# GpSimd's remainders given to VectorE in the latent loop and the band, with the band's sums of exponentials, and the band's casts of weights to ScalarE

## The chip, the core and the metric

The kernel runs on one core of a Trainium2 chip. Its time is the device time of one execution in microseconds (us), the median over runs; lower is better. Five engines work on their own instruction streams and meet at semaphores: TensorE (PE, matmuls; its weight loads are PEld), VectorE (DVE), ScalarE (ACT), GpSimd (POOL) and SyncE (SP, which issues the transfers here). On-chip memory is SBUF; matmuls write into PSUM, in which a "bank" of 512 float32 columns is what one output tile of this kernel holds.

## The reference

A two-layer encoder trunk over 1024 positions of width 1024, all float32. Layer 0 mixes with two groups of heads side by side, layer 1 with a banded attention; each is followed by a SwiGLU feed-forward.

```
layer 0: u = rms_norm(h); proj = u @ w_in -> c_q (384), c_kv (256), k_r (32), q_b, k_b, v_b
  latent:         q_a = rms_norm(c_q) @ w_uq, rotary on the last 32 of 96
                  kv  = rms_norm(c_kv) @ w_ukv; 8 heads; softmax over (s // 64) <= (t // 64)
  stick-breaking: 8 heads of 64, weights from cumulative sums of log_sigmoid(-z)
  h += concat(o_a, o_b) @ w_out
layer 1: 16 heads of 64; each chunk of 64 attends to itself and the 8 before it,
         scores + bias[clip(rel)], softmax, h += o @ w_out
both:    h += (silu(u @ w_gate) * (u @ w_up)) @ w_down        (d_ff 2816), u = rms_norm(h)
end:     rms_norm(h)
```

## The kernel before

**Numbers in two parts.** Every matmul operand is kept as two parts: `hi`, the value rounded to the type fp32r, and `lo`, the remainder, `src - hi` (also fp32r). A product of two such operands is three matmuls (`mm3`, L286 to L291: hi·hi, hi·lo, lo·hi). `split` (L259) makes both parts: `round_to` (L250 to L254) does the rounding as a cast on ScalarE ("act", L252) or VectorE (L254), and `rest` (L256, L257) the subtraction on GpSimd ("pool") or VectorE ("dve"). `weight` (L276) loads a weight by transfer into `wr` tiles of 128x512 and splits it into `wh` and `wl`; each of the three kinds has four buffers. So in the profile L252 and L254 are roundings, and L257 is a remainder, and tile names tell which: `wl<-wr,wh` of weights, `u<-c,u`, `u<-t,u`, `u<-ld,u` of activations.

**Stages.** By the profile's clock: stick-breaking attention to about 415 us (in its last pass, p = 3, the generator `prepare` fills in and makes the first latent tiles); the latent attention loop to about 600; the output projection and the first feed-forward to about 1345, of which 705 to 1290 is in an order written out by hand ("pinned", all on helper line L76) and 1290 to 1345 is its tail, which adds the residual (L719), normalizes (L312, L336, L337) and already loads the band's first weights; the band attention, pairs of heads p = 0 to 7 at about 57 us each, to about 1850, with the output projection's first half (`half(0)`) woven into the last pairs; then the second feed-forward and the end.

**The latent loop** (L1283 to L1302). For each p of 0 to 3, attention of two heads is woven with the projections of the next p: `mla_keys` (L1001) multiplies c_kv's tiles with `w_uk`, scales by a vector into a `c` tile (L1011), splits it (64 rows), and copies the shared rotary key beside it (L1013 on ScalarE, L1014 on VectorE: `lo[64:96] = kc[0:32]`, a cast of 32 rows). `mla_query` (L1017) does the same for queries, with the rotary turn (L997 to L999) into a 96-row `c` tile. `mla_max` (L1048) computes the scores once for their maxima: matmuls L1058 into a two-bank tile `z` (two buffers), whose maximum VectorE takes (L1060), which frees the banks. `mla_attend` (L1111) computes scores again (L1129 to L1131) into the same `z` buffers, ScalarE exponentiates (L1132), and the weighted values go to `o` (L840).

**Sums of exponentials.** `soft_step` (L1065) adds each key block's exponentials to a running tile `b` (L1081): on GpSimd, except where `dest[2]` is set (the last pair of each loop, p = 3 and p = 7), where it is VectorE. `soft_finish` (L1093) sums `b` over partitions by matmuls with ones (L1097), inverts (L1099 to L1102) and scales (L1103).

**The band.** `band_project` (L1139) loads two weights per pair, with the cast on VectorE and the remainder on GpSimd (VectorE for p = 0), and splits the projected `t` tiles on ScalarE and VectorE. `band_max` (L1170) makes scores (L1184) and VectorE adds the bias and takes the maximum in one instruction (L1187, reading and freeing `z`). `band_attend` (L1194) makes scores (L1210, L1211), VectorE adds the bias into an `a` tile (L1212, which frees `z`), ScalarE exponentiates in place (L1213), then the sum (L1081).

**Order.** Outside the pinned part a tile scheduler orders each engine's instructions by its own model when the program is built, and `weave` interleaves attention with filling projections by given costs. So changing an instruction's engine also changes the order round it. An engine runs its instructions in order: one that waits holds up all behind it.

Of the kernel before, what the change touches and what calls it, by code (L numbers as in the profile page):

```python
# [158 lines left out]
class Trunk:  # L159
    def __init__(self, ctx, tc, a):  # L160
# [12 lines left out]
        self.pending = []  # L173
        self.late = []

    def nm(self, s):
        self.n += 1
        return f"{s}{self.n}"
# [77 lines left out]
    def rest(self, eng, lo, src, hi):  # L256
        self.eng(eng).tensor_tensor(lo, src, hi.bitcast(F32), ALU.subtract)  # L257

    def split(self, src, hi, lo, eng_hi="act", eng_lo="pool"):  # L259
        self.round_to(eng_hi, hi, src)  # L260
        self.rest(eng_lo, lo, src, hi)

    def wtile(self, t, part, dt):
        if t:
# [8 lines left out]
            self.nc.sync.dma_start(tiles[-1][:, :w], src[:, c:c + w])  # L273
        return tiles

    def weight(self, src, n=1024, eng_hi="act", eng_lo="pool", into=None, raws=None):  # L276
        parts = []
        for c in range(0, n, HALF):
            w = min(HALF, n - c)
            raw = raws[c // HALF] if raws else self.raws(src[:, c:c + w], w)[0]  # L280
            hi, lo = into[c // HALF] if into else (self.wtile(0, "h", F32R), self.wtile(0, "l", F32R))
            self.split(raw[:, :w], hi[:, :w], lo[:, :w], eng_hi, eng_lo)
            parts.append((hi, lo))
        return Weight(parts)
# [129 lines left out]
    def out_loads(self, o_row, last, parts):  # L414

        for k in range(KD):
            if k != last:
                t, hi, lo = self.load(o_row[k]), self.unit(F32R), self.unit(F32R)
                self.split(t, hi, lo, "act", "pool" if k % 2 else "dve")
                parts[k] = hi, lo  # L420
                yield

    def out_half(self, hf, w, parts, resid, ks, s, h_d, early=0):

        o = [x[0] for x in parts], [x[1] for x in parts]
        ahead, raws, wts = [], [], []
        for m in range(KD):
            while len(ahead) < min(AHEAD, KD - m):
                ahead.append(self.load(resid(hf, m + len(ahead))))
            x, h = ahead.pop(0), self.unit()  # L430
            for n in range(m + len(wts), min(m + early + 1, KD)):
                raw = raws.pop(0) if raws else None
                wts.append(self.weight(w[n], eng_lo="dve" if early else "pool", raws=raw))
            if early and m + early + 1 < KD:
                raws.append(self.raws(w[m + early + 1]))
            ps = self.bank()
            yield from self.dense(ps, wts.pop(0), o, ks)
            self.nc.vector.tensor_tensor(h, ps, x, ALU.add)
            self.nc.sync.dma_start(h_d[hf][m], h)
            s.h[hf].append(h)  # L440
            s.acc[hf] = self.square_sum(s.acc[hf], h)
# [623 lines left out]
    def soft_step(self, lag, scores, cs, st, vt, j, first, last, dest):  # L1065
        x = {}

        def front():
            ex = x["ex"] = self.tmp("a")
            scores(ex)  # L1070
            if first:
                st["ex"] = ex
            else:
                old = st["ex"]
                if "esum" not in st:
                    st["esum"] = self.tmp("b")
                    if cs.start:
                        self.nc.scalar.copy(st["esum"][:, :, 0:cs.start], old[:, :, 0:cs.start])
                else:
                    old = st["esum"]  # L1080
                self.eng("dve" if dest[2] else "pool").tensor_tensor(st["esum"][:, :, cs], old[:, :, cs], ex[:, :, cs],  # L1081
                                                                     ALU.add)

        def back():
            if first:
                st["o"] = self.out_bank()
            self.weighted(st["o"], vt, j, x["ex"], cs, first, last)
            if last:
                self.soft_finish(st["o"], st["esum"], *dest)

        self.step(front, *[lambda: None] * (lag - 1), back)
# [47 lines left out]
    def band_project(self, p, s, out, hfs=(0, 1)):  # L1139

        nc, a = self.nc, self.a
        for i in range(2):
            w = self.weight(a["w_qk1"][2 * p + i], eng_hi="dve", eng_lo="dve" if p == 0 else "pool")
            for hf in hfs:
                ps = self.bank()
                yield from self.dense(ps, w, s.u[hf], range(KD))
                t = self.tmp("t")
                nc.vector.scalar_tensor_tensor(t, ps, 1.0 if i else 0.125, s.r[hf], ALU.mult, ALU.mult)
                for e in range(2):
                    x, y = self.unit(F32R), self.tmp("y", F32R) if i and e == 0 else self.unit(F32R)  # L1150
                    rh = slice(64 * e, 64 * e + 64)
                    rl = slice(64 - 64 * e, 128 - 64 * e)
                    self.split(t[rh, :], x[rh, :], (x[rl, :], y[0:64, :])[i == 0], "act", "dve")
                    if i == 0:
                        nc.sync.dma_start(x[rl, :].bitcast(F32), x[rh, :].bitcast(F32))
                    else:
                        nc.scalar.copy(y[0:64, :], t[rh, :])
                        nc.gpsimd.memset(y[64:68, :].bitcast(F32), 1.0)
                    out[i][e].append((x, y))
# [83 lines left out]
    def mixer0(self, h_d):  # L1243
        nc, a = self.nc, self.a
# [4 lines left out]
        with self.phase("mix0", MIX0_TEMPS):  # L1249
# [5 lines left out]
            raw = [[[], []], [[], []]]  # L1255
# [15 lines left out]
            for p in range(4):  # L1271
                nxt = ([[], []], [[], []], [])
                if p < 2:
                    vw = [a["w_vb"][2], a["w_vb"][3]]
                    fill, cost = self.chain(self.sb_project(p + 1, u, nxt), vgen(vw, 1, [p])), 31.0
                elif p == 2:
                    fill, cost = self.chain(self.sb_project(3, u, nxt), self.rope_key(u)), 31.0
                else:
                    fill, cost = prepare(), 73.0
                self.weave(self.ending(self.sb_attend(p, proj, vts[p], o_d)) if p == 3 else  # L1280
                           self.sb_attend(p, proj, vts[p], o_d), 9.24, fill, cost)
                proj = nxt
            for p in range(4):  # L1283
                nxt = ([[], []], [[], []])
                first, second = (self.mla_attend(p, hf, mla, va[p], o_d) for hf in range(2))
# [19 lines left out]
    def mixer1(self, u, h_d, h2_d):  # L1305
        a = self.a
        o_d = self.spill("o1_")
        out = Stream()
        half = lambda hf, *e: self.out_half(hf, a["w_out1"], o_p[hf], lambda hf, m: h_d[hf][m], list(range(KD)), out,
                                            h2_d, *e)  # L1310
        with self.phase("band", BAND_TEMPS):
            vts = [[] for _ in range(8)]
            vgen = lambda g, hf: self.values([a["w_v1"][2 * g], a["w_v1"][2 * g + 1]], u, 4, KD, 1,
# [185 lines left out]
```

## Time and profile before

| what | value |
|---|---|
| median of 3 runs | 2574.17 us (2573.54 to 2580.01) |
| the profiled execution: time, span | 2573.97 us, 2571.9 us |
| mean granted TensorE clock | 0.993 |
| TensorE busy | 2483.8 us (97%), 11710 matmuls |
| VectorE busy | 1885.4 us (73%), 3074 instructions |
| ScalarE busy | 1170.4 us (46%), 2028 |
| GpSimd busy | 518.1 us (20%), 489 |
| remainders of weights on GpSimd (L257) | 122.9 us, 95, mean 1.299 us |
| sums on GpSimd, `b<-b,a` (L1081) | 110.1 us, 80, mean 1.376 us |

A row of a timeline gives start, duration, engine, line, operation, tiles written and read, shapes and, in brackets, how long the engine had stood idle and what it waited for. A row of a group of instructions gives count, total busy us and mean ns of one, and behind the second bar the idle time before them. Busy times of TensorE are of overlapping matmuls whose ends are modelled.

### The profile page before, as it was taken

Reading aid. Unit: us, or ns where it says so; the run is one execution under the profiler, and the core shown is the slowest. Engines: PE = TensorE matmul, PEld = TensorE weight load, DVE = VectorE, ACT = ScalarE, POOL = GpSimd, SP = SyncE. Lnnn points to the kernel's source line nnn. Section 1 sums busy time; section 2 is a strip of 40 time slices with the busy share of each in tenths; the row PEclk is TensorE's granted clock in tenths of the full one; section 3 lists DMA queues with packets and bytes.
Section 4 is the critical chain, followed back from the end, with each engine's and each line's share of the span. In section 5 each row is a group of like instructions: output and inputs, shape, how many; then the busy total and the mean of one; then the engine's idle time right before and its main releaser. Section 6 shows DMA issues by size and latency. Waiting matters only on the chain.

```text
span 2571.9 us, 33553 instructions
## 1 busy us (share of the span) xinstructions
PE 2483.8 (97%) x11710; PEld 1938.0 (75%) x11710; DVE 1885.4 (73%) x3074; ACT 1170.4 (46%) x2028; POOL 518.1 (20%) x489
## 2 busy tenths in 40 slices
PE   7999998999999999999999999999999999999997
PEld 6766765557778888888878777776777888888886
DVE  6888888666787667677775777777788666667775
ACT  4677676444454344433253344434445443443324
POOL 3333324663000000000031333435300000000004
PEclk9999998999999999999999999999999999999999
DMA  4221100015524343475651222223543433447661
GB/s 140 62 64 54 54 17 29 27 62 164 172 84 150 131 145 125 146 277 184 241 182 54 83 87 80 78 74 111 164 160 116 155 115 131 145 149 255 212 222 70
DMA packets 179432, 319.70 MB, mean 124 GB/s; under 512 B 20544, under 2 KB 36800, under 8 KB 179264
## 3 DMA queue, kind: packets, MB, share of 16 engines
q1 hardware_dynamic: 179264, 317.56, 37.0%
q8 instruction: 93, 1.52, 0.2%
q14 instruction: 75, 0.61, 0.1%
HBM read 222.58 MB, written 84.41 MB: 119 GB/s over the span
## 4 chain that ended last, share of the span: by engine, by line
PE 71%; DVE 10%; DMA 2%; issue 1%; ACT 1%; POOL 0%; DVEq 0%; SPq 0%; POOLq 0%; ACTq 0%
PE z L76 24%; PE mm L76 12%; PE o L76 6%; PE mm L289 5%; PE mm L290 5%; PE mm L291 5%; PE o L840 4%; DVE u L76 2%; PE z L1210 1%; PE z L1184 1%; PE z L1211 1%; DVE u L312 1%; PE z L1097 1%; PE z L1129 1%; DMA wr<-in_w_down 1%
## 5 line engine op out<-in xcount | busy, mean ns | idle before, releaser
L76 PE MATMUL z<-u,wh 128*128 128x512 f32 x976 | 302.3, 390 | 7.1 <-DVE u L76 6.5
L76 PE MATMUL z<-u,vh 128*128 128x512 f32 x976 | 301.7, 390 | 4.0 <-DVE u L76 4.0
L289 PE MATMUL mm<-u,wh 128*128 128x512 f32 x720 | 288.7, 401 | 3.0 <-DVE c L998 1.8
L257 POOL TENSOR_TENSOR wl<-wr,wh 128x512 fp32r<-128x512 f32 (+2 forms) x95 | 122.9, 1299 | 806.8 <-ACT wh L252 739.4
L290 PE MATMUL mm<-u,wh 128*128 128x512 f32 x720 | 284.5, 395 | 0.0
L291 PE MATMUL mm<-u,wl 128*128 128x512 f32 x720 | 282.9, 393 | 0.0
L76 PE MATMUL mm<-u,wh 128*128 128x512 f32 x720 | 223.4, 392 | 4.5 <-ACT wh L76 4.5
L76 PEld LDWEIGHTS z<-u,wh 128*128 128x128 f32 x976 | 183.1, 188 | 48.1 <-DVE u L76 9.4
L76 PEld LDWEIGHTS z<-u,vh 128*128 128x128 f32 x976 | 182.9, 188 | 44.2 <-ACT u L76 5.6
L76 PE MATMUL z<-u,wl 128*128 128x512 f32 x488 | 190.0, 389 | 0.5 <-DVE wl L76 0.5
L76 PE MATMUL z<-u,vl 128*128 128x512 f32 x488 | 189.9, 389 | 0.0
L289 PEld LDWEIGHTS mm<-u,wh 128*128 128x128 f32 x720 | 135.5, 188 | 55.7 <-issue 29.7
L76 PEld LDWEIGHTS mm<-u,wh 128*128 128x128 f32 x720 | 134.7, 188 | 35.5 <-ACT wh L76 6.8
L291 PEld LDWEIGHTS mm<-u,wl 128*128 128x128 f32 x720 | 135.6, 188 | 27.3 <-issue 0.9
L290 PEld LDWEIGHTS mm<-u,wh 128*128 128x128 f32 x720 | 135.8, 189 | 26.7 <-issue 3.0
L840 PE MATMUL o<-a,u 128*64 128x512 f32 (+3 forms) x768 | 155.3, 476 | 0.0
L76 PE MATMUL mm<-u,vh 128*128 128x512 f32 x496 | 152.7, 389 | 0.0
L257 POOL TENSOR_TENSOR u<-wr,u 128x512 fp32r<-128x512 f32 x8 | 10.9, 1373 | 669.5 <-ACT u L252 669.5
L76 PE MATMUL mm<-u,wl 128*128 128x512 f32 x360 | 140.8, 391 | 0.8 <-DVE wl L76 0.5
L1081 POOL TENSOR_TENSOR b<-b,a 128x512 f32<-128x512 f32 (+3 forms) x80 | 110.1, 1376 | 130.0 <-ACT a L1213 101.2
L1212 DVE TENSOR_TENSOR a<-z,bias 128x1024 f32<-128x1024 f32 (+3 forms) x96 | 78.1, 822 | 75.8 <-PE z L1211 70.1
L76 ACT CAST vh<-vr 128x512 fp32r<-128x512 f32 (+1 forms) x166 | 95.8, 577 | 81.3 <-DVE vr L76 30.4
(249 smaller groups left out, 5917.1 us busy)
## 6 DMA issues: line engine op xcount, KB each, us to landing
u<-f_t SPq DMA_DIRECT2D x144, 256.0 KB, 5.0
vr<-in_w_up SPq DMA_DIRECT2D x88, 256.0 KB, 4.5
wr<-in_w_gate SPq DMA_DIRECT2D x88, 256.0 KB, 3.6
f_t<-x SPq DMA_DIRECT2D x72, 256.0 KB, 2.0
wr<-in_w_out SPq DMA_DIRECT2D x64, 256.0 KB, 3.0
f_t<-e SPq DMA_DIRECT2D x54, 256.0 KB, 3.5
ld<-f SPq DMA_DIRECT2D x54, 256.0 KB, 5.1
h<-u SPq DMA_DIRECT2D x48, 256.0 KB, 2.2
```

What stands on the lines that cost most here:

```text
L76: return lambda *a, **k: self.tc.keep_in_program_order(f(*a, **k))
L257: self.eng(eng).tensor_tensor(lo, src, hi.bitcast(F32), ALU.subtract)
L289: mm(out, wh, xh, start=first, stop=False, skip_group_check=onto)
L290: mm(out, wh, xl, start=False, stop=False, skip_group_check=onto)
L291: mm(out, wl, xh, start=False, stop=last, skip_group_check=onto)
L312: self.eng(eng).tensor_tensor(acc, acc, sq, ALU.add)
L840: self.nc.tensor.matmul(o[rh, cs], vt[j // 4][:, j % 4, rh], w[:, e, cs], start=first, stop=last)
L1081: self.eng("dve" if dest[2] else "pool").tensor_tensor(st["esum"][:, :, cs], old[:, :, cs], ex[:, :, cs], ALU.add)
L1097: nc.tensor.matmul(den[64 * e:64 * e + 64, :], self.ones[:, 0:64], esum[:, e, :], start=True, stop=True)
L1129: mm(z[:, e, cs], kth[0:kr, bs], qh[0:kr, cs], start=True, stop=False)
L1184: nc.tensor.matmul(z[:, e, :n], qs[e][hf][0][:, r * P:(r + 1) * P], ks[e][kh][0][:, k0:k0 + n], start=True, stop=True)
L1212: nc.vector.tensor_tensor(ex[:, :, cs], z[:, :, cs], tk[:, :, xs], ALU.add)
```

## The change

Two attributes name the engine of the second part: `second`, the default of `split` and `weight` for the remainder, and `adder`, for the sums. Both begin as GpSimd. Behind the stick-breaking loop `second` becomes VectorE (so `prepare`, which runs in that loop, keeps GpSimd, and the latent sums do too); at the start of the band both become VectorE and stay so to the end, the feed-forward tails and the output projections included. In the band the weights' casts go from VectorE to ScalarE. By the order of the program 206 instructions leave GpSimd for VectorE (92 remainders of weights, 12 of 64 rows and 12 of 96 rows in the latent loop, 20 of tiles for the output projections, and 70 sums), and 36 casts leave VectorE for ScalarE. TensorE and SyncE have the same instructions in partly other order. Line numbers of the changed program are three higher up to the latent loop, four to five higher after it.

```diff
@@ __init__
+        self.second = "pool"
+        self.adder = "pool"
@@ split, weight
-    def split(self, src, hi, lo, eng_hi="act", eng_lo="pool"):
+    def split(self, src, hi, lo, eng_hi="act", eng_lo=None):
         self.round_to(eng_hi, hi, src)
-        self.rest(eng_lo, lo, src, hi)
+        self.rest(eng_lo or self.second, lo, src, hi)
-    def weight(self, src, n=1024, eng_hi="act", eng_lo="pool", into=None, raws=None):
+    def weight(self, src, n=1024, eng_hi="act", eng_lo=None, into=None, raws=None):
@@ out_loads
-                self.split(t, hi, lo, "act", "pool" if k % 2 else "dve")
+                self.split(t, hi, lo, "act", self.second if k % 2 else "dve")
@@ out_half
-                wts.append(self.weight(w[n], eng_lo="dve" if early else "pool", raws=raw))
+                wts.append(self.weight(w[n], eng_lo="dve" if early else None, raws=raw))
@@ soft_step
-                self.eng("dve" if dest[2] else "pool").tensor_tensor(st["esum"][:, :, cs], old[:, :, cs], ex[:, :, cs],
+                self.eng("dve" if dest[2] else self.adder).tensor_tensor(st["esum"][:, :, cs], old[:, :, cs], ex[:, :, cs],
@@ band_project
-            w = self.weight(a["w_qk1"][2 * p + i], eng_hi="dve", eng_lo="dve" if p == 0 else "pool")
+            w = self.weight(a["w_qk1"][2 * p + i], eng_lo="dve")
@@ mixer0, after the stick-breaking loop
+            self.second = "dve"
             for p in range(4):
@@ mixer1, before the band
+        self.second = self.adder = "dve"
         with self.phase("band", BAND_TEMPS):
```

**Three places in VectorE's order.** A row is line, operation, tile written, tiles read, shape; a tile's two numbers tell it from others of its name. The first place is the latent loop, in the second pass (about 478 to 487 us of the profile); m2849 holds a head pair's maxima, z the scores' banks, u506 the shared rotary key, c870 and c873 two heads' scaled keys. Before:

```order
L1011 TENSOR_TENSOR c873_4269<-mm862_4230,u701_3572 64x512
L1060 TENSOR_REDUCE m2849_4192<-z866_4248 128x2
L1060 TENSOR_REDUCE m2849_4192<-z867_4252 128x2
L1014 CAST u869_4260<-u506_2693 32x512
L1014 CAST u872_4268<-u506_2693 32x512
L1060 TENSOR_REDUCE m2849_4192<-z880_4300 128x2
L1060 TENSOR_REDUCE m2849_4192<-z881_4304 128x2
```

In the changed program:

```order
L1063 TENSOR_REDUCE m2849_4192<-z866_4248 128x2
L1063 TENSOR_REDUCE m2849_4192<-z867_4252 128x2
L260 TENSOR_TENSOR u869_4260<-c870_4261,u868_4259 64x512
L1017 CAST u869_4260<-u506_2693 32x512
L1014 TENSOR_TENSOR c873_4269<-mm862_4230,u701_3572 64x512
L1063 TENSOR_REDUCE m2849_4192<-z880_4300 128x2
L260 TENSOR_TENSOR u872_4268<-c873_4269,u871_4267 64x512
L1017 CAST u872_4268<-u506_2693 32x512
L1063 TENSOR_REDUCE m2849_4192<-z881_4304 128x2
```

Each 32-row cast has its remainder (L260) ahead of it, c873's product stands behind the first of them, and one remainder and one cast moved behind the maximum of z880.

The second place is the tail of the first feed-forward (about 1310 to 1316 us); u1930 and u1978 are tiles of the residual sum, u2433 the running sum of squares, wl2471 and wl2478 the remainders of weights for the next stage. Before:

```order
L719 TENSOR_TENSOR u1930_9346<-mm2444_11482,u1930_9346 128x512
L337 SCALAR_TENSOR_TENSOR u2446_11497<-u1930_9346,gains_147,u2445_11496 128x512
L312 TENSOR_TENSOR u2433_11445<-u2433_11445,u2447_11500 128x512
L719 TENSOR_TENSOR u1978_9567<-mm2451_11510,u1978_9567 128x512
L337 SCALAR_TENSOR_TENSOR u2453_11525<-u1978_9567,gains_147,u2452_11524 128x512
L312 TENSOR_TENSOR u2433_11445<-u2433_11445,u2454_11528 128x512
```

In the changed program:

```order
L722 TENSOR_TENSOR u1930_9346<-mm2444_11482,u1930_9346 128x512
L260 TENSOR_TENSOR wl2471_11591<-wr2469_11588,wh2470_11590 128x512
L340 SCALAR_TENSOR_TENSOR u2446_11497<-u1930_9346,gains_147,u2445_11496 128x512
L315 TENSOR_TENSOR u2433_11445<-u2433_11445,u2447_11500 128x512
L722 TENSOR_TENSOR u1978_9567<-mm2451_11510,u1978_9567 128x512
L260 TENSOR_TENSOR wl2478_11619<-wr2476_11616,wh2477_11618 128x512
```

One weight's remainder stands between each residual addition and the step that waits for ScalarE (L340, before L337).

The third place is the band, once per pair; a2946 is a tile of exponentials' arguments, b2933 the running sum, z2948 and z2949 banks of the next maxima. Before:

```order
L1212 TENSOR_TENSOR a2946_14106<-z2947_14107,bias2905_13851 128x2x256
L1101 SCALAR_TENSOR_TENSOR z2943_14095<-z2943_14095,f2944_14098 128x512
L1187 ISA z2948_14115,m22934_14048<-z2948_14115,bias2904_13846 128x384
L1187 ISA m22934_14048 128x1
L1102 SCALAR_TENSOR_TENSOR f2944_14098<-z2943_14095,f2944_14098 128x512
L1187 ISA z2948_14115,m22934_14048<-z2948_14115,bias2904_13846 128x384
```

In the changed program:

```order
L1215 TENSOR_TENSOR a2946_14106<-z2947_14107,bias2905_13851 128x2x256
L1104 SCALAR_TENSOR_TENSOR z2943_14095<-z2943_14095,f2944_14098 128x512
L1084 TENSOR_TENSOR b2933_14045<-b2933_14045,a2946_14106 128x2x256
L1105 SCALAR_TENSOR_TENSOR f2944_14098<-z2943_14095,f2944_14098 128x512
L1190 ISA z2948_14115,m22934_14048<-z2948_14115,bias2904_13846 128x384
L1190 ISA m22934_14048 128x1
L1106 TENSOR_TENSOR f2945_14099<-o2914_13919,f2944_14098 128x512
L1190 ISA z2948_14115,m22934_14048<-z2948_14115,bias2904_13846 128x384
```

The sum (L1084) and the inversion's second step (L1105) now stand ahead of the maximum that frees z2948.

## Prediction

> **What bounds the kernel now.** The page comes first: its total, and the shares of the chain that ended last.
>
> ```profile
> span 2571.9 us, 33553 instructions
> PE 71%; DVE 10%; DMA 2%; issue 1%; ACT 1%; POOL 0%; DVEq 0%; SPq 0%; POOLq 0%; ACTq 0%
> ```
>
> TensorE holds the chain. GpSimd, which loses work, holds none of it; VectorE, which takes the work, holds 10%. So the change can gain only where TensorE waits for a VectorE that GpSimd slows, and lose where VectorE fills up. Busy time by stretch, for the latent loop, the first feed-forward tail, the band pairs and the last pairs with the output projection (columns: stretch, length, then busy time and count of PE, PEld, DVE, ACT, POOL, then granted clock, DMA share, GB/s):
>
> ```profile
> 415.00:600.00 185.00, 173.02 (x744) 104.44 (x742) 138.40 (x170) 88.60 (x142) 111.91 (x79) 0.97 0.17 53
> 485.70:492.40 6.70, 6.17 (x14) 2.40 (x14) 4.60 (x7) 2.73 (x5) 1.95 (x2) 0.50 0.00 0
> 1345.00:1730.00 385.00, 376.61 (x2185) 299.37 (x2186) 273.27 (x590) 152.93 (x272) 132.05 (x132) 1.00 0.25 78
> 1730.00:1850.00 120.00, 119.41 (x574) 82.51 (x571) 90.10 (x187) 52.42 (x89) 59.78 (x50) 1.00 0.43 132
> ```
>
> VectorE and GpSimd are most crowded together in the latent loop (75% and 60%), and only there does the granted clock dip, to 0.50 for 6.7 us. The timeline shows why:
>
> ```profile
> 478.82 1.82 DVE L1060 TENSOR_REDUCE m<-z 128x2 f32<-128x1024 f32 x2
> 480.61 2.71 POOL L257 TENSOR_TENSOR u<-c,u 64x512 fp32r<-64x512 f32 x2
> 483.28 1.26 POOL L1081 TENSOR_TENSOR b<-b,a 128x512 f32<-128x512 f32 x1
> 486.23 1.98 PE L1097 MATMUL z<-b,ones 128*64 128x512 f32 x4 [2.51 <-DVE m L1060]
> ```
>
> The chain of waits has VectorE's pieces between (start, us, what):
>
> ```profile
> 480.68 4.14 DVE u L1014 x2
> 484.85 1.24 DVE m L1060
> ```
>
> Two casts fill 4.14 us, ending just after GpSimd's chain of two remainders and a sum (480.61 to 484.54); the maximum behind them frees the bank TensorE has awaited for 2.51 us. By source line, the same casts and VectorE's other victim (ns min/median/max):
>
> ```profile
> L1014 DVE CAST u<-u x16: 411/1119/2715, 414.0 to 554.5; 32x512 fp32r<-32x512 f32 x16
> L999 DVE TENSOR_TENSOR c<-c,c x12: 682/684/3230, 440.8 to 576.7; 32x512 f32<-32x512 f32 x12
> ```
>
> A cast costs 0.411 us free and 2.715 at worst: GpSimd blocks it for whole instructions.
>
> **The latent loop.** Here 45 remainders go to VectorE; the sums stay on GpSimd. By source line in 415 to 600 (DVE, then POOL), remainders and then sums, and the duration of remainders where VectorE runs four back to back:
>
> ```profile
> 415.00:600.00 185.00, 6.86 (x6) 61.01 (x49) 0.97 0.17 53
> 415.00:600.00 185.00, 2.42 (x3) 51.81 (x30) 0.97 0.17 53
> 736.18 2.41 DVE u L76 x4
> ```
>
> Of the 49, four belong to the preparation and stay. The price is 2.41/4 = 0.60 us each, 45 × 0.60 = +27 us of VectorE. Relief: the 16 casts lasted 19.1 us, the 12 adds of L999 13.9:
>
> ```profile
> L1014 DVE CAST u<-u 32x512 fp32r<-32x512 f32 x16 | 19.1, 1212 | 0.4
> L999 DVE TENSOR_TENSOR c<-c,c 32x512 f32<-32x512 f32 x12 | 13.9, 1162 | 0.4
> ```
>
> At their minima that is 16 × (1.21 - 0.41) + 12 × (1.16 - 0.68) = 18.6 us; GpSimd keeps 46% of its time (51.81 of 111.91), so I take half, 9. VectorE goes to 138 + 27 - 9 = 156 of 185 us.
>
> The stall at 480 to 486: in the new order one remainder stands before each cast, and c873's product (0.68) has moved behind the first. The first maxima end at 480.64, without the product ahead of them at 479.96; then remainder 0.60 (c870, its source, is rounded on ScalarE by then), cast 0.41, product 0.68 and the maximum of 1.24 end at 482.9, before 483.72, where TensorE's wait began (486.23 - 2.51). So the wait goes, and with it the half clock behind it: 6.7 us at 0.50 is 3.35 us lost. Together -5.86 at best, nothing at worst (a sum on GpSimd still in the way); I take -5, near the best, since two of GpSimd's three blocking instructions leave. By the Trainium skill (page "TensorE: Matmul & The Clock Gate", "What's actually happening") the clock halves only after an idle window of about 3.4 us; the row has 0.50 behind an idle of 2.51, so the row decides here, and by the rule alone the term would be at best -2.5.
>
> A second stall, 508 to 513:
>
> ```profile
> 508.44 3.23 DVE L999 TENSOR_TENSOR c<-c,c 32x512 f32<-32x512 f32 x1
> 508.76 2.37 POOL L1081 TENSOR_TENSOR b<-b,a 128x1024 f32<-128x1024 f32 x1
> 513.30 0.51 PE L1129 MATMUL z<-u,u 104*128 104x512 f32 x1 [1.66 <-ACT a L1132]
> ```
>
> The blocker that stays, a sum of 2.37 us, sits across it, so the 1.66 may stay whole: -1.7 to 0, taken -1.0. Against both stands VectorE's extra 27 - 9 = 18 us over the stage. Most hides in its 47 us of idle time; where a remainder stands before a maximum that frees a bank, it shows. And each moved remainder can wait for ScalarE's rounding with the maxima queued behind it; the band's 56 remainders on VectorE (row u<-t below) sat idle 10.6 us for that, 0.19 each, so 8.5 us for 45. Bounds 0 and +9 (a third of 26.5); taken +2.5, nearer the lower, as VectorE still has some 20 us free. Net **-3.5**.
>
> **The first feed-forward tail.** Weight remainders of the next stage move between VectorE's steps:
>
> ```profile
> 1311.93 1.32 DVE L337 SCALAR_TENSOR_TENSOR u<-u,gains,u 128x512 fp32r<-128x512 f32 x1 [0.79 <-ACT u L336]
> 1313.01 1.39 POOL L257 TENSOR_TENSOR wl<-wr,wh 128x512 fp32r<-128x512 f32 x1 [0.31 <-ACT wh L252]
> 1313.17 1.77 DVE L312 TENSOR_TENSOR u<-u,u 128x512 f32<-128x512 f32 x1
> 1315.69 0.47 PE L289 MATMUL mm<-u,wh 128*128 128x512 f32 x1 [1.04 <-DVE u L719]
> ```
>
> GpSimd stretches L337 and L312; the residual addition behind them comes 1.04 us late. The moved remainder (0.60) falls into the 0.79 us in which VectorE awaits ScalarE, and nothing stretches any more. Bounds -2.5 (this and the stage's smaller waits) and 0; taken **-1.5**.
>
> **The band.** Per pair, ten sums move: one of 1024 columns, three each of 768, 512 and 256. VectorE already does some for the last pairs:
>
> ```profile
> L1081 DVE TENSOR_TENSOR b<-b,a 128x1024 f32<-128x1024 f32 x3 | 3.8, 1269 | 5.9 <-ACT a L1132 5.9
> L1081 DVE TENSOR_TENSOR b<-b,a 128x768 f32<-128x768 f32 x3 | 3.3, 1103 | 3.7 <-ACT a L1213 2.2 <-ACT a L1132 1.6
> L1081 DVE TENSOR_TENSOR b<-b,a 128x512 f32<-128x512 f32 x5 | 3.6, 718 | 2.2 <-ACT a L1132 1.2 <-ACT a L1213 1.0
> L1081 DVE TENSOR_TENSOR b<-b,a 128x256 f32<-128x256 f32 x5 | 2.5, 491 | 3.4 <-ACT a L1132 2.4 <-ACT a L1213 1.0
> ```
>
> 1.27 + 3 × (1.10 + 0.72 + 0.49) = 8.2 us a pair; 58 of the 70 lie in 1345 to 1730, so 5.8 × 8.2 = +48. Of weights and remainders in that stretch:
>
> ```profile
> 1345.00:1730.00 385.00, 0.00 (x0) 82.87 (x58) 1.00 0.25 78
> L257 POOL TENSOR_TENSOR wl<-wr,wh 128x512 fp32r<-128x512 f32 x24 | 31.6, 1324 | 53.3 <-DVE wh L254 52.8 <-PE z L1184 0.6
> L254 DVE CAST wh<-wr 128x512 fp32r<-128x512 f32 x29 | 20.2, 696 | 22.6 <-PE mm L291 19.1 <-PE mm L290 3.5
> L252 ACT CAST wh<-wr 128x512 fp32r<-128x512 f32 x26 | 16.1, 618 | 12.0 <-PE mm L290 9.7 <-POOL b L1081 2.1
> L257 DVE TENSOR_TENSOR u<-t,u 64x512 fp32r<-64x512 f32 x56 | 46.5, 831 | 11.5 <-ACT u L252 10.6
> ```
>
> 24 remainders cost +14; 29 casts go to ScalarE (-20 on VectorE, 29 × 0.618 = +18 there, 153 to 171 of 385: no cost, its idle time hides it; without that cover each weight would come 0.62 late, and the exponentials queued behind a cast that awaits its buffer with it, as behind the 26 that stand there now); the 56 remainders fall from 0.83 towards 0.60 to 0.69 (-8 to -13). VectorE: 273 + 48 + 14 - 20 - 10 = 305 of 385, 79%. The average has room. Each pair has two tight places:
>
> ```profile
> 1608.90 1.31 DVE L257 TENSOR_TENSOR u<-t,u 64x512 fp32r<-64x512 f32 x1 [1.34 <-ACT u L252]
> 1610.72 0.44 PE L1210 MATMUL z<-u,u 128*128 128x384 f32 x1 [1.20 <-DVE a L1212]
> 1594.60 2.35 DVE L1212 TENSOR_TENSOR a<-z,bias 128x1024 f32<-128x1024 f32 x2
> 1601.74 0.96 DVE L1212 TENSOR_TENSOR a<-z,bias 128x768 f32<-128x768 f32 x1 [3.34 <-PE z L1211]
> ```
>
> First, TensorE waits 1.20 us behind the addition that follows a stretched remainder (1.31, against 0.60 to 0.69 free): a gain of up to 1.20 in each of 7 pairs, -8.4. Second, VectorE runs full up to 1597; there a 512 sum (0.72) now stands before the maximum of z2948, and a 768 sum (1.10) further on: +1.82 a pair, +12.7, if nothing covers it. The new order puts 29 instead of 22 of TensorE's filling matmuls before the bank in question, and VectorE is idle 3.34 us soon after. These ends lie about evenly round nothing: **0**.
>
> **The rest.** In 1730 to 1850 (remainders by source line, DVE, then POOL)
>
> ```profile
> 1730.00:1850.00 120.00, 14.90 (x18) 40.33 (x30) 1.00 0.43 132
> ```
>
> 30 remainders (30 × 0.60 = 18 us) come to a VectorE busy 90 of 120: bounds -1 and +4, taken **+0.5**. The second feed-forward tail and the end gain or lose what can't be told from 0. Sum: -3.5 - 1.5 + 0 + 0.5 = -4.5. The profiled execution took 2573.97 us, 2.1 more than its span and 0.2 below the median of 2574.17, so **2569.5**. About 0.3%, 7.7 us, is what a measurement of this kernel can tell from no change; the forecast lies inside.
>
> **Rivals.**
> *The gain is larger (0.28, faster).* The waits all go, nothing is given back: -5.9 - 1.7 - 2.5, and half of the band's wait, -4.2: 14.3 less, 2559.7. For it: the same blocking stands in each row above. Against: VectorE is 75% busy already and gets 18 us more.
> *VectorE becomes the bound in the band (0.16, slower).* One mechanism: sums queued before maxima and bias additions that free TensorE's banks, uncovered from the point at which a pair's sums in the full stretch exceed the filling matmuls. Price 12.7 on the other terms: 2574.0 - 4.5 + 12.7 = 2582.2. Against: 29 matmuls of filling.
> *The remainders inherit the blocking (0.10).* The 30 sums on GpSimd last 51.81/30 = 1.73 us and fill 28% of the latent loop; a moved remainder that meets one waits half of it: 45 × 0.28 × 0.86 = 10.9 us. All on the path: 2569.5 + 10.9 = 2580.4. For it: L999 lasted 3.23 beside a sum of 2.37. By the Trainium skill ("SBUF — State Buffer", "Who interferes with whom") a VectorE instruction with two SBUF inputs contends with a GpSimd one that reads SBUF, and moved remainders are such; L999's row agrees.
> That the change does nothing is ruled out: 206 instructions leave GpSimd and 36 casts leave VectorE.
>
> **Numbers.** Forecast 0.46 (0.36 same, 0.08 faster, 0.02 slower); larger gain 0.28 faster; band 0.16 slower; inherited blocking 0.10 (0.08 same, 0.02 slower). Faster 0.36, same 0.44, slower 0.20. The range 2557 to 2584 takes in the rivals' values; the forecast's own bounds are some 2564 to 2575.
>
> **What would show it.** Right: no wait before L1097's counterpart near 480, granted clock 1.00 there; casts of 32 rows at 0.41; VectorE near 305 in the band; the waits of 1.04 in the tail and 1.20 in each pair smaller. Wrong: a new wait of TensorE on a VectorE maximum in the band, once per pair; remainders of 64 rows at well over 1 us beside sums; TensorE waiting for a weight's remainder that VectorE took up late.

## The result and the profile after

The changed kernel takes 2599.81 us (median of 4 runs, 2598.2 to 2601.02) against 2574.24: 1.0097 times as long, with a 95% interval of 1.0079 to 1.0114. On another chip it was 2597.91 against 2575.01, 1.009 (1.0065 to 1.0114). The prediction said 2569.5, in a range up to 2584: wrong in size and in sign.

The changed kernel's page, its total, busy times and the chain that ended last:

```profile
span 2599.3 us, 33426 instructions
PE 2507.9 (96%) x11710; PEld 1952.8 (75%) x11710; DVE 1968.1 (76%) x3244; ACT 1191.2 (46%) x2064; POOL 244.1 (9%) x283
PE 71%; DVE 10%; DMA 2%; issue 2%; ACT 1%; DVEq 0%; SPq 0%; ACTq 0%
```

The work moved as told: GpSimd from 518 to 244 us, VectorE from 1885 to 1968, less than what it took over, since some of what it had before got shorter (the band's 56 remainders `u<-t` took 46.5 us and now take 38.4). The shares of the chain look as before. Where the time went has to be read stage by stage. Both programs issue 11710 matmuls, so the start of the matmul with the same number gives the lead or lag at each place. TensorE's order differs in parts, so this is good to some tenths of a us. What each stage adds, in us against the profile of before (the stage's bounds are those of before):

| stage | change after | the same, second profile |
|---|---|---|
| 0 to 415, stick-breaking | -0.6 | -0.8 |
| 415 to 604, latent loop | +18.8 | +13.3 |
| 604 to 1290, projection and pinned feed-forward | +1.2 | -1.3 |
| 1290 to 1345, the feed-forward's tail | -3.3 | -3.3 |
| 1345 to 1729, band pairs | +4.7 | +4.9 |
| 1729 to 1840, last pairs and output projection | +6.2 | +7.6 |
| 1840 to the end | +0.7 | +1.1 |

So three stages answer for it, and the latent loop, of which the prediction expected a gain, for more than half.

**The latent loop.** TensorE's waits by releaser in the changed kernel: the list's first row is one that before did not have (us in total, times, longest).

```profile
PE z L1061 <- DVE f L1105: 11.5, 3, 4.8
```

The stretch of the loop, and five microseconds inside it (columns as in the prediction's windows):

```profile
415.00:620.00 205.00, 183.80 (x750) 111.69 (x749) 167.82 (x218) 89.67 (x142) 57.63 (x34) 0.91 0.15 48
520.00:525.00 5.00, 5.00 (x16) 2.72 (x12) 0.97 (x2) 1.12 (x2) 2.79 (x2) 0.50 0.34 108
```

TensorE is idle for 205.00 - 183.80 = 21.2 us, where it was idle for 12.0 (185.00 - 173.02); that is half of the loss. The other half is clock: the mean is 0.91 instead of 0.97, and each of the three waits is followed by a stretch like 520 to 525 at 0.50. The timeline before the longest wait:

```profile
570.65 0.70 DVE L1104 SCALAR_TENSOR_TENSOR z<-z,f 128x512 f32<-128x512 f32 x1
571.05 2.34 POOL L1084 TENSOR_TENSOR b<-b,a 128x1024 f32<-128x1024 f32 x1 [0.72 <-ACT a L1135]
571.38 2.56 DVE L260 TENSOR_TENSOR u<-c,u 64x512 fp32r<-64x512 f32 x1
573.87 0.67 DVE L1105 SCALAR_TENSOR_TENSOR f<-z,f 128x512 f32<-128x512 f32 x1
574.60 0.69 PE L1061 MATMUL z<-u,u 104*128 104x128 f32 x2 [4.81 <-DVE f L1105]
```

A moved remainder (L260) stands between the two steps of the inversion (L1104, L1105). It starts 0.33 us behind one of the sums that stayed on GpSimd and ends just after it: 2.56 us for work of 0.68. L1105 is what releases the bank that TensorE's next maximum needs, so TensorE stands still. At the other two waits (3.38 us, ending at 463.98, and 3.31 us) no remainder stands inside the inversion; there the stretched ones stand ahead of it. The second of them:

```profile
512.19 0.63 ACT L1103 ACTIVATE f<-f 128x512 f32<-128x512 f32 x1
513.87 2.38 POOL L1084 TENSOR_TENSOR b<-b,a 128x1024 f32<-128x1024 f32 x1 [1.70 <-ACT a L1135]
514.63 1.90 DVE L260 TENSOR_TENSOR wl<-wr,wh 128x256 fp32r<-128x256 f32 x1
516.56 0.70 DVE L1104 SCALAR_TENSOR_TENSOR z<-z,f 128x512 f32<-128x512 f32 x1
518.75 0.69 PE L1061 MATMUL z<-u,u 104*128 104x128 f32 x2 [3.31 <-DVE f L1105]
```

ScalarE has the inversion's input ready at 512.82, and VectorE takes it up at 516.56, 3.7 us later; at the other two places it is 4.5 and 4.8 us. Over the whole loop all ten remainders, both additions L1002 and both casts that began while a sum ran ended 0.28 to 0.55 us behind the end of that sum, whereas products that read one of their inputs from PSUM (L1001, two cases) kept their 0.69 us beside it. What the sums do to VectorE over the whole loop (groups of instructions, changed kernel, window 415 to 605):

```profile
L260 DVE TENSOR_TENSOR u<-c,u 64x512 fp32r<-64x512 f32 x12 | 13.0, 1087 | 0.3
L1017 DVE CAST u<-u 32x512 fp32r<-32x512 f32 x15 | 12.6, 843 | 0.2
L1002 DVE TENSOR_TENSOR c<-c,c 32x512 f32<-32x512 f32 x12 | 12.4, 1032 | 0.4
L260 DVE TENSOR_TENSOR wl<-wr,wh 128x384 fp32r<-128x384 f32 x7 | 7.9, 1145 | 0.1
```

**The tail** ran without a pause of TensorE; the window from 1290 to 1345, before and then after:

```profile
1290.00:1345.00 55.00, 52.17 (x229) 41.93 (x228) 38.45 (x54) 28.22 (x47) 22.38 (x22) 1.00 0.59 189
```
```profile
1290.00:1345.00 55.00, 55.00 (x242) 44.96 (x241) 42.03 (x70) 25.03 (x42) 2.24 (x8) 1.00 0.68 223
```

**The last pairs.** TensorE's timeline near the output projection, before:

```profile
1807.39 0.96 PE L1184 MATMUL z<-u,u 128*128 128x128 f32 x4
1808.18 0.45 PE L289 MATMUL mm<-u,wh 128*128 128x512 f32 x1
...
1809.40 0.40 PE L291 MATMUL mm<-u,wl 128*128 128x512 f32 x1
1809.63 0.64 PE L1184 MATMUL z<-u,u 128*128 128x256 f32 x4
1810.11 0.39 PE L289 MATMUL mm<-u,wh 128*128 128x512 f32 x1
```

and in the changed kernel:

```profile
1834.54 0.96 PE L1187 MATMUL z<-u,u 128*128 128x128 f32 x4
1835.34 0.45 PE L294 MATMUL mm<-u,wl 128*128 128x512 f32 x1
1836.66 0.75 PE L1187 MATMUL z<-u,u 128*128 128x256 f32 x4 [0.87 <-DVE m L1190]
1838.61 1.33 PE L1187 MATMUL z<-u,u 128*128 128x384 f32 x4 [1.21 <-DVE m L1190]
```

The maxima's matmuls need banks that VectorE frees. Before, six or seven of the projection's matmuls stood between two groups of them and covered that; in the new order of TensorE there is one behind the first group and none behind the second, and the wait shows. Ahead of this place is another new wait, of 2.11 us, for the pair's output to be split on VectorE.

### The profile page after: what moved, and what is told of

It reads as the page before. It is cut to its first block, busy times and chain, and to the rows that moved or that the text cites. A ratio compares the mean times of both kernels' runs of the same rounds, so it can differ in the third digit from the quotient of the medians.

```text
span 2599.3 us, 33426 instructions
## 1 busy us (share of the span) xinstructions
PE 2507.9 (96%) x11710; PEld 1952.8 (75%) x11710; DVE 1968.1 (76%) x3244; ACT 1191.2 (46%) x2064; POOL 244.1 (9%) x283
## 4 chain that ended last, share of the span: by engine, by line
PE 71%; DVE 10%; DMA 2%; issue 2%; ACT 1%; DVEq 0%; SPq 0%; ACTq 0%
PE z L76 24%; PE mm L76 12%; PE o L76 6%; PE mm L292 6%; PE mm L294 6%; PE mm L293 6%; PE o L843 4%; DVE u L76 2%; PE z L1187 1%; PE z L1213 1%; PE z L1214 1%; PE z L1100 1%; PE z L1061 1%; DMA wr<-in_w_down 1%; DVE z L1190 1%
## 5 line engine op out<-in xcount | busy, mean ns | idle before, releaser
L292 PEld LDWEIGHTS mm<-u,wh 128*128 128x128 f32 x720 | 135.9, 189 | 54.5 <-issue 27.3
L843 PE MATMUL o<-a,u 128*64 128x512 f32 (+3 forms) x768 | 163.0, 487 | 0.6 <-ACT a L1216 0.6
L255 ACT CAST wh<-wr 128x512 fp32r<-128x512 f32 (+1 forms) x159 | 95.9, 605 | 116.2 <-PE mm L293 85.5
L260 DVE TENSOR_TENSOR wl<-wr,wh 128x512 fp32r<-128x512 f32 (+1 forms) x170 | 123.6, 732 | 27.5 <-ACT wh L255 25.5
L76 ACT CAST wh<-wr 128x512 fp32r<-128x512 f32 (+1 forms) x190 | 109.5, 583 | 35.8 <-DVE wr L76 29.3
L76 DVE TENSOR_TENSOR wl<-wr,wh 128x512 fp32r<-128x512 f32 (+1 forms) x190 | 120.7, 642 | 2.9 <-ACT wh L76 2.9
```

Of the source, the lines that this page charges most:

```text
L76: return lambda *a, **k: self.tc.keep_in_program_order(f(*a, **k))
L255: self.nc.scalar.copy(hi, src)
L292: mm(out, wh, xh, start=first, stop=False, skip_group_check=onto)
L843: self.nc.tensor.matmul(o[rh, cs], vt[j // 4][:, j % 4, rh], w[:, e, cs], start=first, stop=last)
```

## The experiments

Stage values are worked out as in the table above; ratios are against runs of the kernel before on the same chip. The kernel before itself ran from 2568.97 to 2583.37 us there, more widely than in the first four runs; why is in the last section.

**Latent loop alone, band alone.** The changed kernel with the one or the other undone.

```diff
@@ latent alone: mixer1, band_project
-        self.second = self.adder = "dve"
+        self.second = self.adder = "pool"
-            w = self.weight(a["w_qk1"][2 * p + i], eng_lo="dve")
+            w = self.weight(a["w_qk1"][2 * p + i], eng_hi="dve", eng_lo="dve" if p == 0 else "pool")
@@ band alone: mixer0
-            self.second = "dve"
```

> The change in the latent loop alone; from the band on everything is as before (remainders and sums on GpSimd, weight casts of the band on VectorE). If the stages add up, as the comparison of the two traces says (+18.2 us from 415 to 620 of the profile, the rest after it), this takes 2574.2 + 18 = 2590 to 2594 us. If the loss comes from how the stages hang together (buffers, transfers running ahead), it lands far from that, below 2584 or above 2599.

> The change from the band on alone; the latent loop keeps its remainders on GpSimd. If the stages add up: 2599.8 - 18.2 = 2580 to 2584 us, with the first feed-forward's tail 3.3 us shorter than before, each pair of the band 0.6 to 0.7 us longer, and about 6 us lost in the output projection near 1810. If most of the loss were the latent loop's and the rest a shift of it, it takes 2574 us or less.

Measured: latent alone 2588.11 us, 1.0042 (1.0027 to 1.0057), band alone 2585.68, 1.004 (1.0026 to 1.0053). By stages: latent alone +12.5 in the loop, -3.3 in the tail, nothing in the band; band alone nothing in the loop, +5.6 in the pairs to 1800, +6.5 from there to 1840. The parts add up: 11.2 + 8.8 = 20 of the 23 to 26 us. One expectation was wrong: in band alone the tail gained 0.5, not 3.3. The tail's weights are those of its own down projection (`wr<-in_w_down`), generated while the latent loop's setting holds, not the band's, as the prediction had it.

**What in the latent loop: the blocking, or the load?** First the 30 sums on VectorE as well, so that GpSimd, behind the preparation's last remainders (to about 420 us), reads nothing; then GpSimd kept busy with fills into the same tiles, which read nothing. For this second kernel the order of VectorE's and of TensorE's instructions is the same, row for row, as in the changed kernel; what it leaves out is the softmax denominators of the first three pairs.

```diff
@@ sums on VectorE too: mixer0
-            self.second = "dve"
+            self.second = self.adder = "dve"
@@ fills in the sums' place: soft_step
+                if dest[2] or self.adder == "dve":
+                    nc = self.nc
+                    nc.vector.tensor_tensor(st["esum"][:, :, cs], old[:, :, cs], ex[:, :, cs], ALU.add)
+                else:
+                    self.nc.gpsimd.memset(st["esum"][:, :, cs], 1.0)
```

> The changed kernel with the latent loop's 30 sums on VectorE as well, so that GpSimd reads nothing there. Theory A, blocking: the three waits of 3.3 to 4.8 us behind the inversion come from VectorE being held by GpSimd's sums; without them the remainders take 0.6 to 0.7 us, the waits shrink below 1.5 us each and the time is 2574 to 2585 us, though VectorE has 30 instructions more. Theory B, load: VectorE has too many instructions; 30 sums of about 0.9 us are 27 us more on it, and the time grows to 2605 to 2625 us.

> The changed kernel in which the latent loop's sums on GpSimd are fills with a constant into the same tiles (for the first three pairs the softmax denominators are left out of the computation); VectorE's instructions are those of the changed kernel. Theory A, blocking by reads of GpSimd: VectorE runs at its free durations (64-row remainders 0.69 us against 1.09, 32-row casts 0.41 against 0.84), the three long waits go, 2572 to 2582 us. Theory B, load: the waits stay, 2595 to 2600 us. If GpSimd blocks whatever it does, the durations stay stretched wherever a fill runs.

Measured: with fills 2581.76 us, 1.0024 (1.0009 to 1.0039), and in the loop -1.5 us, where the changed kernel lost 18.8 and 13.3. With the sums on VectorE 2589.26, 1.0051 (1.0033 to 1.007), the loop +7.7. Groups of the kernel with fills, and below them its timeline beside a run of seven fills:

```profile
L260 DVE TENSOR_TENSOR u<-c,u 64x512 fp32r<-64x512 f32 x12 | 8.2, 682 | 0.7 <-ACT u L255 0.5
L1017 DVE CAST u<-u 32x512 fp32r<-32x512 f32 x14 | 9.3, 667 | 0.2
L1002 DVE TENSOR_TENSOR c<-c,c 32x512 f32<-32x512 f32 x12 | 8.2, 683 | 0.4
L1088 POOL MEMSET b<- 128x1024 f32 x12 | 11.4, 950 | 42.5 <-PE z L1103 27.7 <-ACT u L1030 14.4
```
```profile
500.60 5.73 POOL L1088 MEMSET b<- 128x1024 f32 x7 [14.40 <-ACT u L1030]
501.26 0.63 ACT L1106 ACTIVATE f<-f 128x512 f32<-128x512 f32 x1
501.82 0.43 DVE L260 TENSOR_TENSOR wl<-wr,wh 128x256 fp32r<-128x256 f32 x1
502.28 0.70 DVE L1107 SCALAR_TENSOR_TENSOR z<-z,f 128x512 f32<-128x512 f32 x1
503.01 0.68 DVE L1002 TENSOR_TENSOR c<-c,c 32x512 f32<-32x512 f32 x1
504.38 0.69 DVE L260 TENSOR_TENSOR u<-c,u 96x512 fp32r<-96x512 f32 x1
```

Theory A holds: with VectorE's and TensorE's instructions in the same order, it is what GpSimd does beside them that makes the difference of 15 to 20 us in the loop (by the ratios of the whole time, 1.0097 and 1.009 against 1.0024, 17 to 19 us). The timeline shows the place of the second long wait: the seven fills run through the whole inversion, the remainder ahead of it takes 0.43 us instead of 1.90, the inversion starts 0.4 us after ScalarE's input instead of 3.7, and TensorE doesn't wait. So at this place it is that the sum reads, and not that GpSimd is busy, which holds VectorE. It is a bound, not a version, since a fill can't replace a sum. Fills are shorter (0.95 us against 2.4), wait for less and so run in bunches; near the third place none ran, so for the whole loop it isn't separated how much of the 15 to 20 us is the reading and how much the shorter time. Casts met fills only twice. One began 0.2 us before a fill's end and took 0.47 us; the other, behind a remainder on GpSimd, took 3.85:

```profile
416.64 2.54 POOL L260 TENSOR_TENSOR u<-f,u 64x512 fp32r<-64x512 f32 x2 [4.01 <-ACT u L255]
419.13 7.21 POOL L1088 MEMSET b<- 128x1024 f32 x10
418.08 3.85 DVE L1017 CAST u<-u 32x512 fp32r<-32x512 f32 x1
```

With the sums on VectorE the time lies between the ranges of both theories. Remainders and additions are not stretched (0.68 us), and yet the loop loses 7.7, with TensorE waiting for maxima (9.4 us in five waits, PE z L1045 on DVE L1043). So theory B had something too; but the order changed with the sums, and load and order aren't separated here.

**The changed kernel again**, as a control.

> The changed kernel itself, beside the three below on one chip. If the parts add up (latent loop alone +11, band alone +9 as measured), it lies some 20 to 26 us above the kernel before; if the parts share a cost, below 15.

Measured: 2597.91 us, given above, 22.9 above the kernel before, as expected if the parts add up; the three latent waits were 3.38, 3.30 and 1.76 us.

**The parts of the band's change.** All with the latent loop as before: the band without its sums, without its casts, the sums alone, the casts alone, and the band with the remainders from the last pair on given back.

```diff
@@ without sums: mixer1
-        self.second = self.adder = "dve"
+        self.second = "dve"
@@ without casts: band_project
-            w = self.weight(a["w_qk1"][2 * p + i], eng_lo="dve")
+            w = self.weight(a["w_qk1"][2 * p + i], eng_hi="dve", eng_lo="dve")
@@ sums alone: mixer1 (band_project's weights as before)
+        self.second, self.adder = "pool", "dve"
@@ casts alone: mixer1, band_project
+        self.second = self.adder = "pool"
+            w = self.weight(a["w_qk1"][2 * p + i], eng_lo="dve" if p == 0 else "pool")
@@ remainders given back: mixer1, p == 7
+                    self.second = "pool"
```

> The band's change without its sums: remainders on VectorE and casts on ScalarE, sums on GpSimd; the latent loop as before. Theory S: the 0.8 us lost in each band pair are the sums that stand before maxima and bias additions on VectorE; without them a pair takes its 57.3 us as before, and the wait of 1.20 us per pair is there again, since a sum on GpSimd stretches the remainder before it; 5 to 6 us less than the band's change alone, so 2 to 5 us above the kernel before. Theory R: the loss comes from the casts on ScalarE and the remainders of weights; each pair keeps its 0.8 us.

> The band's change without its casts, which stay on VectorE (20 us more there). Theory S (sums and the order that they bring): as the band's change alone, 8 to 10 us above the kernel before, or a little more. If the casts on ScalarE cost, 3 us or less above it.

> The kernel before with the band's 70 sums on VectorE and nothing else. Theory S: nearly the whole loss of the band's change: 0.6 to 0.9 us a pair, and 6 us in 1800 to 1840, where the scheduler puts one or two filling matmuls instead of seven to nine between the four maxima's; 9 to 12 us above the kernel before. If sums and remainders share the loss, 4 to 6 us.

> The kernel before with the band's 36 casts of weights on ScalarE, and nothing else. By the forecast's step and by theory S it is the same as the kernel before, within 2 us: TensorE's order in the last pairs keeps its filling matmuls between the maxima's. If the casts move TensorE's order, 2 to 7 us slower, in 1800 to 1840.

> The band's change alone, with remainders given back to GpSimd from the last pair on (output projection and second feed-forward's tail). If the 6.5 us near 1810 come from VectorE taking the output projection's remainders beside the last pair's maxima, they go: the wait of 2.1 us before the projection's first product and the two of 0.8 and 1.2 us before the maxima's matmuls vanish, and the kernel lies 2 to 4 us above the one before. If they come from the sums, it stays 8 to 10 us above.

| kernel | time, us | ratio (95%) | 1345 to 1729 | 1729 to 1840 |
|---|---|---|---|---|
| band alone | 2585.68 | 1.004 (1.0026 to 1.0053) | +4.6 | +7.5 |
| without sums | 2579.67 | 1.0019 (1.0007 to 1.003) | +1.7 | +4.1 |
| without casts | 2586.04 | 1.0039 (1.0023 to 1.0055) | +4.0 | +7.4 |
| sums alone | 2588.54 | 1.0057 (1.0035 to 1.0079) | +4.3 | +10.8 |
| casts alone | 2575.09 | 0.9999 (0.9988 to 1.001) | -0.2 | +0.2 |
| remainders given back | 2586.38 | 1.0043 (1.0028 to 1.0058) | +4.7 | +8.8 |

The sums alone cost at least as much as everything together, more than the 9 to 12 us expected, and the casts nothing; theory S holds for the pairs in the main (4.3 of 4.6), though without the sums there is a loss of 1.7 too. The remainders given back gained nothing: the kernel stayed above the one before, by 11.4 us, a little more than the 8 to 10 expected for that case. So taking that load off VectorE does not remove the loss near 1810. There, without the sums, the wait of 2.11 us shrinks to 0.23, but the two before the maxima's matmuls stay:

```profile
1810.64 0.74 PE L292 MATMUL mm<-u,wh 128*128 128x512 f32 x2 [0.23 <-DVE u L257]
1814.30 0.76 PE L1187 MATMUL z<-u,u 128*128 128x256 f32 x4 [0.88 <-DVE m L1190]
1816.26 1.33 PE L1187 MATMUL z<-u,u 128*128 128x384 f32 x4 [1.20 <-DVE m L1190]
```

So sums bring one wait (of 2.11 us; with the sums alone 1.5), and either the sums or the remainders (with the casts) bring the scheduler to the order of TensorE that has one or no matmul between the first three groups of the maxima's. With the casts alone seven or eight stand there, much as before, and the time is the old one.

In the pairs the loss has no single place. The wait of 1.20 us, which TensorE had six times before (7.2 us), is gone, and in band alone all of TensorE's waits from 1345 to 1732 add up to 1.3 us; still the stage is 4.6 us longer. One place looks like a new wait. Band alone, once per pair:

```profile
1537.82 1.40 DVE L1047 TENSOR_TENSOR u<-z,scalars 4x512 fp32r<-4x512 f32 x2
1538.60 1.07 PE L843 MATMUL o<-a,u 128*64 128x512 f32 x2
1539.60 0.19 PEld L1214 LDWEIGHTS z<-u,y 68*128 68x128 f32 x1 [0.81 <-DVE u L1047]
```

The kernel before at the same place:

```profile
1535.23 1.40 DVE L1044 TENSOR_TENSOR u<-z,scalars 4x512 fp32r<-4x512 f32 x2
1535.45 0.39 PE L291 MATMUL mm<-u,wl 128*128 128x512 f32 x1
...
1536.15 0.40 PE L1211 MATMUL z<-u,y 68*128 68x512 f32 x1
```

But the 0.81 us is idle time of the weight load (PEld); TensorE's own row has none. Both orders have three of the projection's matmuls between the maxima's transposition (L1042, L1045) and the first product with the row that VectorE writes (L1211, L1214). Band alone has two matmuls of weighted values (L843) there as well, and 2.47 us pass instead of 1.38. With the sums left on GpSimd it is 1.37, so this comes with the sums; some 0.5 of the extra 1.1 us is work that moved here from elsewhere.

An estimate from the starts of the matmuls, with the usual 0.226 us for one of 512 columns, divides the stage's +4.6: 6.0 us are won ahead of the scores' matmuls, where the wait of 1.20 was, some 3 are lost ahead of the maxima's matmuls, and some 6 among and behind the weighted values and the sums over partitions, by wider spacing in pieces of mostly less than 0.3 us; the rest is small. Whether these losses come from the new order or from the sums' own time on VectorE is open, and so is whether an order with the sums on VectorE and TensorE's fill left in place would gain: the order comes out of the scheduler with the engines, and no kernel held it fixed.

**Versions that might beat both.** The tail's remainders alone on VectorE, and that with the latent loop's sums (remainders left on GpSimd).

```diff
@@ tail alone: mixer0, behind the latent loop (its own setting removed); mixer1 and band_project as before
                 mla = nxt
+            self.second = "dve"
@@ with the latent sums: mixer0, ahead of the latent loop
+            self.adder = "dve"
```

> The kernel before, with the remainders of the first feed-forward's tail alone (16 of w_down's) on VectorE. All traces with these there show the stage from 1290 to 1345 3.3 us shorter and none of the three waits of 1.04, 1.32 and 0.47 us; so 3 us less than the kernel before, which is less than its runs scatter. If those 3.3 us came from the latent loop's change in some other way, no gain at all.

> The other half given to VectorE in the latent loop: its 30 sums, with the remainders left on GpSimd; the first feed-forward tail's remainders on VectorE as well, the band as before. If it is the length of one GpSimd instruction that decides (2.4 us for a sum, 1.3 for a remainder), the waits of the latent loop shrink and the kernel is 3 to 6 us faster than the one before, the best of all. If VectorE's load decides, the loop loses as much as with both on VectorE (7.7 us in one trace) and the kernel is 3 to 6 us slower.

Measured: 2573.19 us, 0.9993 (0.9983 to 1.0004), and 2574.55, 1.0001 (0.9991 to 1.0011). Both have the tail's -3.3 us and no wait of TensorE there. In time that can't be told from no change; the latent loop's scatter (last section) is larger. The second kernel's loop came out at +4.8, within that scatter, and shows neither the gain nor the loss that was expected clearly. Nothing found here is measurably faster than the kernel before.

## Why the prediction was wrong

**The latent stall (-5): right.** Between 480 and 505 of the clock of before the changed kernel regains 6.8 us on the kernel before, the 2.51 wait is gone, and the clock from there to 510 is full.

**The second stall (-1.0): right in size.** The 1.66 wait became 0.31, which is 1.3 us less. But 5 us behind it stands one of the three new waits, of 3.31 us, at a maximum that didn't wait before.

**Given back (+2.5, bounds 0 and +9): this step failed.** It measured about 21 to 27 (the loop's 13.3 or 18.8 plus what the stalls gave, 6.8 and 1.3). Three things were wrong in it. It reckoned with averages: VectorE at 156 of 185, 84%, which is what came (167.8 of 205, 82%); but the loss is made in three places where stretched remainders keep VectorE from the inversion that frees a bank, twice from ahead of it and once from inside. It took the moved remainders at 0.60 us; beside GpSimd's sums those of 64 rows take 1.09 on the mean and up to 2.77. That is the sign of being wrong that the prediction itself had named, remainders of 64 rows at well over 1 us beside sums. And it priced a wait at its length, although the prediction itself had read that a wait of 2.51 us cost 3.35 more in half clock: the three waits of 11.5 us in all came with about as much again.

**The rival that named it.** "The remainders inherit the blocking" had the mechanism, a chance of 0.10 and a price of 10.9 us; the runs give 15 to 20 (changed kernel against fills). It was priced as waiting time spread over VectorE, not as a stalled bank with half clock behind it. The forecast itself used the opposite, a relief of half of 18.6 us, though the sums, the longer of GpSimd's instructions, were to stay.

**The tail (-1.5): right mechanism, too small.** -3.3: all of its waits went (1.04, 1.32 and 0.47 us, 2.8 in all), not only the one behind the stretched steps. Whose weights they are was wrong, as told above.

**The band (0, bounds -8.4 and +12.7): +4.7.** Both terms were in part right. VectorE's busy time came out near the forecast (297.8 us in the matching 388.7, 305 of 385 forecast), and the wait of 1.20 us went; there were six of these, 7.2 us, not seven. The other bound, maxima held up by sums at 1.82 us a pair, is there in small: by the estimate above some 3 us in the whole stage. The some 6 us round the weighted values and the sums over partitions stood in no term. The prediction had compared TensorE's order at one place, where the fill grew from 22 to 29 matmuls, and not elsewhere.

**The last pairs (+0.5, bounds -1 and +4): +6.2 to +7.6, outside the bounds.** It counted 18 us of remainders on VectorE; giving them back gained nothing (+8.8 against +7.5), while the sums alone cost 10.8. What the sum lacked is TensorE's new order, in which the maxima's matmuls lose their cover (0.87 and 1.21 us), and the wait of 2.11 us for the pair's output.

**The casts (0): right**, 0.9999 (0.9988 to 1.001).

## What to carry to other kernels

Before work is moved from GpSimd to VectorE, look at what stays on GpSimd: in this loop each sum there held the VectorE instructions with two inputs in SBUF that began beside it until its own end (2.56 us for work of 0.68), and moving half of the work only put more instructions of VectorE under the other half. Price a moved instruction by what it is queued in front of, above all by the instruction that frees a bank, and price a wait of TensorE with the half clock behind it. Where a scheduler sets the order, compare TensorE's order at every place that waits in the profile of before or has short cover, and not only where the fill grew: near the output projection six or seven covering matmuls became one and none.

## What was not expected of the hardware

**The price of the same wait differs from run to run.** The latent loop of the kernel with the casts alone is that of the kernel before, and it has the same wait of TensorE there, 2.50 us against the 2.51 of the prediction's row:

```profile
485.39 1.60 PE L1100 MATMUL z<-b,ones 128*64 128x512 f32 x4 [2.50 <-DVE m L1063]
```

Behind it, the window from 490 to 510, before and then casts alone:

```profile
490.00:510.00 20.00, 20.00 (x78) 10.90 (x78) 12.80 (x17) 8.87 (x14) 9.07 (x7) 0.94 0.08 26
```
```profile
490.00:510.00 20.00, 20.00 (x72) 11.09 (x71) 10.94 (x15) 7.27 (x12) 7.23 (x6) 0.85 0.08 26
```

The half clock lasted longer: six matmuls fewer were done here. Near 424 us there are 6.8 us of half clock where before had 3.4, and a stretch from 550.7 to 554.1 has no counterpart before. The loop took 4.2 us more, and in the kernel with the tail's remainders alone, whose loop is that of the kernel before as well, 4.1. Casts alone, where before was at 1.00 again from 492.5 on:

```profile
485.90:495.90 10.00, 10.00 (x22) 4.17 (x19) 5.39 (x8) 2.73 (x5) 1.95 (x2) 0.50 0.07 26
```

By the clock's records in the traces every stretch at 0.50, but for the last one at the end of each program, lasts 3.4, 6.8 or 10.2 us, in all fourteen traces. Between 415 and 604 they add up to 10.2 us before and to 20.5 in casts alone, and to 37.5 and 27.3 in the two profiles of the changed kernel. At 0.50 a stretch costs at most half its length, so a difference of 10.2 us at most 5.1. That can account for the 4.2 us above and for most of the 5.5 between +18.8 and +13.3. The same shows in the whole time of the kernel before: over 63 runs on the later chips the mean granted clock goes from 0.989 to 0.994, and the median times at these two ends are 2580.6 us (2 runs) and 2569.5 (5 runs). What decides how many steps of 3.4 us a wait brings is not shown.

**What VectorE does not lose.** By the Trainium skill ("SBUF — State Buffer", "Who interferes with whom") a VectorE instruction with two SBUF inputs contends with a GpSimd instruction that reads SBUF, not with one that only writes it. The kernel with fills agrees: 0.43 to 0.69 us for remainders and additions beside fills, where sums made four groups of them 1.03 to 1.21 on the mean. The same section lets casts contend as well, where their operands allow a mode that uses both ports, and has whoever issues second wait for the whole instruction. The two casts beside fills fit that: the one of 3.85 us, which outlasted a remainder, and the one of 0.47 us each ended some 0.28 us behind the end of a fill; they are two cases.
